# Expert layer of a two-block network: one-hots of two tokens side by side, an earlier first split, gate loads tied to weight loads, and padding between tiles

## The chip, the cores and the metric

The kernel runs on one core of one Trainium2 chip. The metric is the device time of one launch in microseconds (us). A core has a matrix engine (TensorE, PE in the profile; PEld is its loading of stationary operands), a vector engine (VectorE, DVE), a scalar engine (ScalarE, ACT), GpSimd (POOL), and the queue from which nearly all transfers are issued (SyncE, SP). Each works through its own list of instructions in order; semaphores tie the lists together. Operands lie in an on-chip memory of 128 partitions (SBUF); an address below is a byte offset within a partition. Sums of products land in a second memory, PSUM.

## The reference, cut to what matters

256 tokens of width 1024 pass first through two layers of attention and a gated MLP, then through two layers of a second kind: a mixing sublayer and a layer of 16,384 experts ("PEER"). Everything is float32. The change lies in the expert layer:

```
q      = xn @ wq                       # 8 heads x 2 halves x 128
scores = q . sub_keys                  # 128 keys per half
16 best of each half -> 16 best of the sums -> expert numbers idx = 128*i + j, gate = softmax
act    = xn . u_tab[idx]               # 8 x 16 experts per token
y      = sum over them of gelu(act) * gate * v_tab[idx]
```

The kernel does not gather rows. It computes the products with all 16,384 rows of U, multiplies gelu of them by a table of gates that is zero for experts not chosen, and multiplies the result by all rows of V.

## The kernel before, in words

**Weights.** Every large matrix comes in pieces of 128 x 1024 floats. `weights` (line 146) issues one transfer of 512 KB into one of three buffers `wx`, ACT rounds it to a short float `wh` (`split`, line 140) and DVE subtracts to get the rest `wl`; there are four buffers of each. A product x*w is three matmuls: high by high, low by high, high by low (`mm3`, line 134). PE, ACT and DVE work on different pieces; a buffer is written again when PE has read it. Transfers are issued from the SP queue in one order, so a transfer that waits for its buffer holds up those behind it.

**The expert layer (`peer`, line 1036).** After the choice of experts has begun (`select`, line 1187), U is done in two halves of 32 steps. A step (`u_step`) takes two pieces of U: 2 x 8 blocks x 3 = 48 matmuls, each with a 128 x 128 block of the piece as the stationary operand and 256 tokens as the moving one. ACT takes gelu of the sums into `at0` (first half) or `at1` (second). Beside the first half the rest of the choice runs (`rank`), woven in by `weave`.

**Gates.** For tokens 0 to 127 the gates are scattered by POOL into a table in HBM (`scatter_gates`, line 202), which has been cleared by 64 writes from a tile of zeros (`clear_gates`); later it comes back in 64 loads of 128 KB (`load_gates`, line 220), and DVE multiplies `at` by each. For tokens 128 to 255 they are built on the chip, four tokens at a time, in 32 builds (`build`): DVE compares a row of 0 to 127 with the chosen i (tile `oi`) and j (`oj`), multiplies `oj` by three parts of the gate (`og`), and for each of the four tokens PE multiplies `oi` by `og` in three bf16 matmuls of 128 x 128. The four tokens are interleaved: a token's column lies every fourth element, 8 bytes apart. DVE multiplies `at0` and what there is of `at1` by the result; ACT copies the rest to `at1`, and a later `u_step` multiplies its gelu by it (tile `y`). In the second half of U every step is followed by one build.

**V.** After the last build `first_split` loads two gates, multiplies, and splits the first chunk of `at` into `eh` and `el`; then 64 steps `v_step` follow, each with two pieces of V and 2 x 4 x 3 = 24 matmuls, with 128 x 128 of `eh` or `el` stationary and 512 columns of `wh` or `wl` moving. In the middle of a step `v_split` prepares the next chunk and asks for the gate two chunks on. The framework under the kernel orders each engine's list itself, by what could be ready; only stated dependencies bind it. The gate loads depend on the scatter and on a free buffer out of three.

**Where tiles lie.** Pools are laid out one after the other from both ends, the tiles of a pool in the order of their first use. By the sizes in the code, with the addresses that the program was given: `wx` from 20704, `wh` from 32992, `wl` from 49376, each buffer 4096 long, so every buffer of weights starts at 32 modulo 64. In the expert layer `xh` and `xl` (8 blocks of 256 floats, 1024 bytes each) start at 212960 and 221152, also 32 modulo 64, and `eh`, `el` of V too. In the second mixing sublayer `yh` starts at 113376 in layer 0 (32 modulo 64) and at 111616 in layer 1 (0 modulo 64); in the first block's MLP `gh` and `gl` start at 0 modulo 64.

Of the kernel before, what the change touches and what calls it, by code (L numbers as in the profile page):

```python
# [20 lines left out]
T = 256  # L21
# [26 lines left out]
OUT_ORDER = (4, 6, 7, 3, 0, 1, 5, 2)  # L48
WX, WH, WL = 3, 4, 4

# [5 lines left out]
LAG, TAIL, AHEAD, HOLD = 4, 2, 2, (2, 6)  # L56
SIDE_Q, SIDE_S = 2500, 2800
UQ_SIZES = [768, 512]
# [3 lines left out]
class Net:  # L62
    def __init__(self, tc, a, out, ctx, dbg=None):
        self.tc, self.nc, self.a, self.out, self.dbg = tc, tc.nc, a, out, dbg or {}
        self.n = 0
        self.queue = []
        self.act_set, self.act_pre, self.act_ops = None, None, []
        pool = tc.tile_pool
        self.cp = ctx.enter_context(pool(name="cp", bufs=1))
        self.wp = ctx.enter_context(pool(name="wp", bufs=1))  # L70
        self.gctx = ctx
        self.pp = ctx.enter_context(pool(name="pp", bufs=1, space=bass.MemoryType.PSUM))
        self.big = [self.pp.tile([128, 2, T], F32, name=f"big{b}", tag=f"big{b}", bufs=1) for b in range(4)]
# [391 lines left out]
    def out_tokens(self, units, first, last, then=None):  # L465

        for b in range(4):
            tk, s = slice(b % 2 * 128, b % 2 * 128 + 128), slice(b // 2 * 512, b // 2 * 512 + 512)
            for n, ((h, l), (xh, xl)) in enumerate(units):
                end = last and n == len(units) - 1  # L470
                self.mm(self.bank(b), xh[:, tk], h[:, s], first and n == 0, False)
                self.mm(self.bank(b), xl[:, tk], h[:, s], False, False)
                self.mm(self.bank(b), xh[:, tk], l[:, s], False, end)
            if then is not None:
                then(b)
# [560 lines left out]
    def peer(self, l):  # L1036
# [3 lines left out]
        with ExitStack() as ctx:  # L1040
            ip = ctx.enter_context(self.pool("pi"))
            idx = self.t(ip, [128, 128], U32, tag="idx")
            gs = [self.t(ip, [128, 8, 16], tag=f"gs{tt}") for tt in range(2)]
            iT, jT = (self.t(ip, [128, 128], BF16, tag=n) for n in ("iT", "jT"))
            gT = self.t(ip, [128, 3, 128], BF16, tag="gT")
            io = self.t(ip, [128, 128, 4], BF16, tag="io")
            for _ in self.clear:
# [20 lines left out]

            def build(g):


                t0, done = 124 - 4 * g, 2 * g + 2
                oi, oj = (self.t(self.op, [128, 128, 4], BF16, tag=n, bufs=2) for n in ("oi", "oj"))
                og = self.t(self.op, [128, 3, 128, 4], BF16, tag="og", bufs=2)
                self.tt(oi, io, iT[:, None, t0:t0 + 4].to_broadcast([128, 128, 4]), OP.is_equal)
                self.tt(oj, io, jT[:, None, t0:t0 + 4].to_broadcast([128, 128, 4]), OP.is_equal)
                self.tt(og, oj[:, None].to_broadcast([128, 3, 128, 4]),
                        gT[:, :, None, t0:t0 + 4].to_broadcast([128, 3, 128, 4]), OP.mult)
                yield 1900
                ps = self.ps([128, 4, 128])  # L1080
                for k in range(4):
                    for n in range(3):
                        self.mm(ps[:, k], oi[:, :, k], og[:, n, :, k], k == 0 and n == 0, n == 2)
                ps = ps.rearrange("p t j -> p j t")
                t0 += 128
                a0, a1 = at0[:, :, t0:t0 + 4], at1[:, :, t0:t0 + 4]
                self.tt(a0, a0, ps[:, :64], OP.mult)
                self.tt(a1[:, :done], a1[:, :done], ps[:, 64:64 + done], OP.mult)
                if done < 64:
                    self.copy(a1[:, done:], ps[:, 64 + done:])  # L1090
                yield 700

            parts, loaded = {}, {}

            def g_load(n):
                if n < 64:
                    loaded[n] = self.load_gates(l, n, early)

            def v_split(n, pool):

                if n < 64:
                    g_load(n + 2)
# [3 lines left out]
                    self.split(h, low, a)  # L1106
                    parts[n] = [(h[:, m], low[:, m]) for m in range(2)]

            def first_split():
                for n in range(2):  # L1110
                    g_load(n)
                v_split(0, early)

# [26 lines left out]
            with self.pool("pn") as npool:  # L1140
# [5 lines left out]
                self.xctx.close()  # L1146
                self.open_xs()
                pool = sctx.enter_context(self.pool("pk", "right"))
# [7 lines left out]
                self.copy(io16, it[:, 0:16, None].to_broadcast([128, 16, 128]))  # L1156
                self.copy(io, it[:, :, None].to_broadcast([128, 128, 4]))
# [12 lines left out]
            self.hctx.close()  # L1170
# [8 lines left out]
            vctx = ExitStack()  # L1179
            vp = vctx.enter_context(self.pool("pv", "right"))  # L1180
            for half, at in enumerate((at0, at1)):
                weave(lambda jp: v_step(at, jp, half), iter(()), 0)
            vctx.close()
        if l < DEPTH - 1:
            self.open_xs()

    def select(self, l, pool, w, lead, normed, io16, gs, idx, turned):
# [63 lines left out]
        def rest_of_ranks():  # L1251
            yield from normed
            pend.sort(key=lambda x: x[0])
            for tt in range(2):
# [15 lines left out]
                bt = best[tt]  # L1270
                g = gs[tt]
                self.tt(g, bt, bt[:, :, 0:1].to_broadcast([128, 8, 16]), OP.subtract)
# [265 lines left out]
```

## Time and profile before

| what | value |
|---|---|
| median of 2 runs | 2615.31 us (2614.23 to 2616.39) |
| the profiled execution, its own time | 2614.9 us |
| its span, first to last instruction | 2613.0 us |
[...]
| PE busy / DVE busy / ACT busy / POOL busy | 2560.8 / 1835.9 / 1383.7 / 463.4 us |
| transfers | 470.95 MB, 180 GB/s over the span |

A matmul's recorded duration includes the pipeline, and matmuls overlap: what a matmul costs is the distance of its start from the next one's. The chain of waits shows this best: it merges a run of matmuls into one line with its length and count, and length by count is the distance. The lines of a helper such as `mm` (L132), `copy` (L118) and `tt` (L121) carry many different operations; the names behind them tell which.

### The profile page before, as it was taken

Reading aid. Unit: us, or ns where it says so; the run is one execution under the profiler, and the core shown is the slowest. Engines: PE = TensorE matmul, PEld = TensorE weight load, DVE = VectorE, ACT = ScalarE, POOL = GpSimd, SP = SyncE. Lnnn points to the kernel's source line nnn. Section 1 sums busy time; section 2 is a strip of 40 time slices with the busy share of each in tenths; the row PEclk is TensorE's granted clock in tenths of the full one; section 3 lists DMA queues with packets and bytes.
Section 4 is the critical chain, followed back from the end, with each engine's and each line's share of the span. In section 5 each row is a group of like instructions: output and inputs, shape, how many; then the busy total and the mean of one; then the engine's idle time right before and its main releaser. Section 6 shows DMA issues by size and latency. Waiting matters only on the chain.

```text
span 2613.0 us, 46153 instructions
## 1 busy us (share of the span) xinstructions
PE 2560.8 (98%) x18042; PEld 2366.2 (91%) x18042; DVE 1835.9 (70%) x3511; ACT 1383.7 (53%) x2128; POOL 463.4 (18%) x261
## 2 busy tenths in 40 slices
PE   8999999999999999999999999999999999999999
PEld 7799997999999999999878888999999999878887
DVE  6688777877887995666665555877994666675555
ACT  6565566655676554444444444776554443344443
POOL 0000000000000077773000000000178772000000
PEclk9999999999999999999999999999999999999999
DMA  8756652566535576665576666635576665676664
GB/s 281 235 179 192 183 174 79 153 192 183 175 116 185 170 185 186 149 150 149 193 249 203 194 194 193 185 107 187 173 191 179 148 150 148 212 248 194 194 194 158
DMA packets 195098, 470.95 MB, mean 180 GB/s; under 512 B 54644, under 2 KB 89588, under 8 KB 193856
## 3 DMA queue, kind: packets, MB, share of 16 engines
q1 hardware_dynamic: 158016, 467.86, 56.9%
q0 software_dynamic: 36864, 0.15, 3.6%
q8 instruction: 141, 2.31, 0.3%
q14 instruction: 77, 0.63, 0.1%
HBM read 447.86 MB, written 20.05 MB: 179 GB/s over the span
## 4 chain that ended last, share of the span: by engine, by line
PE 85%; DMA 6%; DVE 6%; ACT 2%; issue 1%; SPq 0%; ACTq 0%; DVEq 0%
PE pj L132 46%; PE big L132 31%; PE ps L132 7%; DMA gate<-gates 4%; DVE wl L121 2%; DMA wx<-in_w 1%; ACT wh L118 1%; PE ps L573 1%; DVE el L121 1%; DVE xn L124 0%; DVE at L121 0%; DVE xT L121 0%; DMA wx<-in_wq 0%; DVE xl L124 0%; DVE c L124 0%
## 5 line engine op out<-in xcount | busy, mean ns | idle before, releaser
L118 ACT ACTIVATE wh<-wx 128x1024 fp32r<-128x1024 f32 (+1 forms) x800 | 844.4, 1057 | 898.7 <-PE pj L132 356.1
L121 DVE TENSOR_TENSOR wl<-wx,wh 128x1024 fp32r<-128x1024 f32 (+1 forms) x800 | 975.0, 1220 | 453.8 <-ACT wh L118 446.4
L132 PE MATMUL pj<-xh,wh 128*128 128x256 f32 x3136 | 897.3, 286 | 10.5 <-ACT wh L118 7.9
L132 PE MATMUL pj<-xl,wh 128*128 128x256 f32 x3136 | 889.6, 284 | 3.3 <-DVE xl L124 2.7
L132 PE MATMUL pj<-xh,wl 128*128 128x256 f32 x3136 | 889.1, 284 | 3.8 <-DVE wl L121 3.8
L209 POOL DMA_INDIRECT gates<-gs,idx x256 | 462.9, 1808 | 1712.6 <-DVE idx L129 1591.8
L132 PEld LDWEIGHTS pj<-xh,wh 128*128 128x128 f32 x3136 | 601.2, 192 | 12.8 <-ACT wh L118 8.3
L132 PEld LDWEIGHTS pj<-xl,wh 128*128 128x128 f32 x3136 | 600.5, 191 | 7.9 <-DVE xl L124 6.5
L132 PEld LDWEIGHTS pj<-xh,wl 128*128 128x128 f32 x3136 | 599.9, 191 | 6.6 <-DVE wl L121 5.7
L132 PE MATMUL big<-wh,el 128*128 128x512 f32 x1024 | 402.1, 393 | 10.4 <-DVE el L121 10.3
L132 PE MATMUL big<-wh,eh 128*128 128x512 f32 x1024 | 400.0, 391 | 11.6 <-ACT eh L118 11.6
L132 PE MATMUL big<-wl,eh 128*128 128x512 f32 x1024 | 399.9, 390 | 0.0
L132 PEld LDWEIGHTS big<-wh,el 128*128 128x128 f32 x1024 | 193.1, 189 | 58.4 <-DVE el L121 19.2
L132 PEld LDWEIGHTS big<-wh,eh 128*128 128x128 f32 x1024 | 193.0, 189 | 52.6 <-ACT eh L118 12.2
L132 PEld LDWEIGHTS big<-wl,eh 128*128 128x128 f32 x1024 | 193.1, 189 | 39.6
L121 DVE TENSOR_TENSOR at<-at,ps 128x256 f32<-128x256 f32 (+20 forms) x128 | 45.1, 352 | 131.6 <-PE ps L132 131.6
L132 PE MATMUL ps<-og,oi 128*128 128x128 bf16 x768 | 101.5, 297 | 0.0
L132 PE MATMUL big<-gh,wh 128*128 128x256 f32 x352 | 99.1, 282 | 0.0
L132 PE MATMUL big<-gl,wh 128*128 128x256 f32 x352 | 98.9, 281 | 0.0
L132 PE MATMUL big<-gh,wl 128*128 128x256 f32 x352 | 98.8, 281 | 0.0
L121 DVE TENSOR_TENSOR at<-at,gate 128x256 f32<-128x256 f32 x128 | 52.9, 422 | 58.4 <-DMA gate<-gates 58.0
L121 DVE TENSOR_TENSOR el<-at,eh 128x512 fp32r<-128x512 f32 x128 | 87.2, 684 | 0.0
(355 smaller groups left out, 3309.0 us busy)
## 6 DMA issues: line engine op xcount, KB each, us to landing
wx<-in_u SPq DMA_DIRECT2D x256, 512.0 KB
wx<-in_v SPq DMA_DIRECT2D x256, 512.0 KB
wx<-in_wm SPq DMA_DIRECT2D x132, 512.0 KB
wx<-in_w SPq DMA_DIRECT2D x88, 512.0 KB
gates<-zero SPq DMA_DIRECT2D x128, 128.0 KB
wx<-in_wo SPq DMA_DIRECT2D x32, 512.0 KB
wx<-in_wq SPq DMA_DIRECT2D x32, 512.0 KB
gate<-gates SPq DMA_DIRECT2D x128, 128.0 KB
```

Of the source, the lines that this page charges most:

```text
L118: return self.nc.scalar.activation(out, in_, AF.Copy)
L121: return self.nc.vector.tensor_tensor(out, a, b, op=op)
L132: return self.nc.tensor.matmul(ps, w, x, start=start, stop=stop, skip_group_check=True)
L209: d = self.nc.gpsimd.indirect_dma_start(flat, IndirectOffsetOnAxis(ap=idx[:, p:p + 1], axis=0), g[:, p:p + 1], None, compute_op=OP.add).ins
L573: self.nc.tensor.transpose(tp[:, kt, qt * 128:(qt + 1) * 128], p[:, qt, kt * 128:(kt + 1) * 128], self.ident)
```

## The change

- **Interleaving.** The one-hots hold two pairs of two tokens, [128, 2, 128, 2], so that a token's column lies every second element, 4 bytes apart; `og` is made in two halves. The numbers of instructions: one DVE multiplication more per build, the same 12 matmuls.
- **Order.** The builds are a generator `builds`, woven into the second half of U like `rank` into the first, at 3100 ns of work per step (a build yields 2750); `pairs` and `built` count what is done. gelu of the tokens that have a gate already is now written back to PSUM and multiplied from there. When the builds are through, `first_split` follows in the same weave, with gate 0 in a tile of its own; gates 1 and 2 are asked for when V begins.
- **Gate loads** get a dependency on the last weight load before them in the program (`fetched`), which orders them behind it in the SP queue.
- **Padding.** A lead of 288 bytes before `wx`, `zero` half as large (its copies read it twice), each pair of weight buffers a tag of its own with 32, 32, 64, 0 bytes behind `wl`; 64 bytes behind each of the 8 blocks of `xh` and `xl` in the expert layer, and 480 or 448 bytes above them; `eh`, `el` in blocks of 136 floats, 544 bytes; 32 bytes above V's pool. By the same rule of layout `wx` then starts at 20480 and the four pairs `wh`, `wl` at 0, 32, 64 and 128 modulo 512; `xh` starts at 211456 in layer 0 (0 modulo 64) and at 211488 in layer 1 (32 modulo 64), with blocks 1088 bytes apart. Tiles of the left pools move down by 96 bytes.

```diff
+LEAD, PADS = 288, (32, 32, 64, 0)
+VP = (32, 32)
-SIDE_Q, SIDE_S = 2500, 2800
+SIDE_Q, SIDE_S, SIDE_G = 2500, 2800, 3100
...
+        self.t(self.wp, [128, LEAD // 4], tag="lead")
...
-            self.nc.sync.dma_start(x[:, :tot], ap[:, off:off + tot])
+            self.fetched = self.nc.sync.dma_start(x[:, :tot], ap[:, off:off + tot]).ins
...
-                h = self.t(self.wp, [128, 1024], F32R, tag="wh", bufs=WH)
-                l = self.t(self.wp, [128, 1024], F32R, tag="wl", bufs=WL)
+                b = self.units % 4
+                h, l = (self.t(self.wp, [128, 1024 + n // 4], F32R, tag=x + "abcd"[b]) for x, n in (("wh", 0), ("wl", PADS[b])))
+                self.units += 1
...
-        self.zero = self.t(self.cp, [128, 2, 128], tag="zero")
+        self.zero = self.t(self.cp, [128, 128], tag="zero")
...
-            self.nc.sync.dma_start(self.gates[l][:, j:j + 2], self.zero)
+            self.nc.sync.dma_start(self.gates[l][:, j:j + 2], self.zero[:, None].to_broadcast([128, 2, 128]))
...
-        g = self.t(pool, [128, 2, 128], tag="gate", bufs=3)
+        g = pool if n == 0 else self.t(pool, [128, 2, 128], tag="gate", bufs=3)
         d = self.nc.sync.dma_start(g, self.gates[l][:, 2 * n:2 * n + 2]).ins
+        self._dep(d, self.fetched)
...
-    def open_xs(self):
+    def open_xs(self, gap=0, below=0):
...
-        self.xh, self.xl = (self.t(pool, [128, 8, T], F32R, tag=n) for n in ("xh", "xl"))
+        self.xh, self.xl = (self.t(pool, [128, 8, T + gap // 4], F32R, tag=n)[:, :, :T] for n in ("xh", "xl"))
+        if below:
+            self.t(pool, [128, below // 4], tag="below")
...
-            def u_step(at, jp, tb=0):
+            def u_step(at, jp):
...
-                a = at[:, 2 * jp:2 * jp + 2]
-                self.act(a[:, :, :T - tb], ps[:, :, :T - tb], AF.Gelu_apprx_tanh)
-                if tb:
-                    y = self.t(self.op, [128, 2, 128], tag="y", bufs=2)[:, :, :tb]
-                    self.act(y, ps[:, :, T - tb:], AF.Gelu_apprx_tanh)
-                    self.tt(a[:, :, T - tb:], a[:, :, T - tb:], y, OP.mult)
+                a, n = at[:, 2 * jp:2 * jp + 2], T - built[0]
+                self.act(a[:, :, :n], ps[:, :, :n], AF.Gelu_apprx_tanh)
+                if built[0]:
+                    self.act(ps[:, :, n:], ps[:, :, n:], AF.Gelu_apprx_tanh)
+                    self.tt(a[:, :, n:], a[:, :, n:], ps[:, :, n:], OP.mult)
-            def build(g):
...
+            def builds(pairs):
+                for t0 in range(124, -1, -4):
+                    oi, oj = (self.t(self.op, [128, 2, 128, 2], BF16, tag=n, bufs=b) for n, b in (("oi", 2), ("oj", 1)))
+                    chosen = lambda x: x[:, t0:t0 + 4].rearrange("p (a t) -> p a t", t=2)[:, :, None].to_broadcast([128, 2, 128, 2])
+                    for o, x in ((oi, iT), (oj, jT)):
+                        self.tt(o, io[:, None].to_broadcast([128, 2, 128, 2]), chosen(x), OP.is_equal)
+                    ps = self.ps([128, 4, 128])
+                    for a in range(2):
+                        og = self.t(self.op, [128, 3, 128, 2], BF16, tag="og", bufs=2)
+                        self.tt(og, oj[:, a:a + 1].to_broadcast([128, 3, 128, 2]),
+                                gT[:, :, None, t0 + 2 * a:t0 + 2 * a + 2].to_broadcast([128, 3, 128, 2]), OP.mult)
+                        for k in range(2):
+                            for n in range(3):
+                                self.mm(ps[:, 2 * a + k], oi[:, a, :, k], og[:, n, :, k], a == 0 and k == 0 and n == 0,
+                                        n == 2)
+                    yield 2000
...
+                    built[0] += 4
+                    yield 750
...
-                    h, low = (self.t(pool, [128, 2, T], F32R, tag=x, bufs=1 + (n > 0)) for x in ("eh", "el"))
+                    h, low = (self.t(pool, [128, 2, 2, 136], F32R, tag=x, bufs=1 + (n > 0))[:, :, :, :128] for x in ("eh", "el"))
...
-                for g in range(32):
-                    u_step(at1, g, 4 * g)
-                    for _ in build(g):
-                        pass
-            early = ctx.enter_context(self.pool("pf"))
-            first_split()
+                weave(u_second, builds(pairs), SIDE_G, first_split)
...
+            for n in (1, 2):
+                g_load(n)
```

## Rows read from the trace of the kernel before

**Rows 1.** Page, part 1: each engine's busy time, share, instructions.
```profile
PE 2560.8 (98%) x18042; PEld 2366.2 (91%) x18042; DVE 1835.9 (70%) x3511; ACT 1383.7 (53%) x2128; POOL 463.4 (18%) x261
```

**Rows 2.** Chain of waits: start us, length us, what; the expert layers.
```profile
862.38 126.00 PE pj L132 x1050
...
1053.47 5.75 PE pj L132 x48
1059.22 1.43 PE ps L132 x12
...
1373.81 265.28 PE big L132 x1169
```

**Rows 3.** Windows: stretch, its length, busy us of each engine, clock, DMA share, GB/s.
```profile
1053.00:1268.00 215.00, 215.00 (x1800) 213.14 (x1798) 142.98 (x237) 87.94 (x150) 119.34 (x72) 1.00 0.59 148
1268.00:1374.00 106.00, 94.58 (x430) 75.95 (x428) 70.94 (x116) 44.34 (x54) 0.00 (x0) 0.97 0.76 243
1374.00:1640.00 266.00, 266.00 (x1178) 220.42 (x1178) 149.69 (x149) 129.70 (x148) 0.00 (x0) 1.00 0.62 196
```

**Rows 4.** Timeline of PE, U's last matmul to V's first in layer 0.
```profile
1274.32 0.28 PE L132 MATMUL pj<-xh,wl 128*128 128x256 f32 x1
1274.45 1.58 PE L132 MATMUL ps<-og,oi 128*128 128x128 bf16 x12
1281.82 1.22 PE L132 MATMUL big<-wh,eh 128*128 128x512 f32 x2 [5.80 <-ACT eh L118]
1282.84 0.63 PE L132 MATMUL big<-wh,el 128*128 128x512 f32 x1
1283.27 0.63 PE L132 MATMUL big<-wl,eh 128*128 128x512 f32 x1
1283.69 0.63 PE L132 MATMUL big<-wh,el 128*128 128x512 f32 x1
```

**Rows 5.** Waits and the queue's own, 1268 to 1374: total us, times, longest.
```profile
DVE at L121 <- DMA gate<-gates: 29.3, 24, 3.0
PE big L132 <- DVE el L121: 5.6, 8, 1.8
...
SPq L154 <- DVE at L121: 16.2, 14, 1.5
```

**Rows 6.** Chain of waits, V's beginning and steady part in layer 1; a gate's landing.
```profile
2243.97 5.50 DMA gate<-gates
...
2250.64 12.90 PE big L132 x47
...
2342.22 266.66 PE big L132 x1175
```

**Rows 7.** Groups by line, 1053 to 1268: count, busy us, mean ns, idle before.
```profile
L132 PEld LDWEIGHTS pj<-xh,wh 128*128 128x128 f32 x480 | 91.8, 191 | 0.0
L121 DVE TENSOR_TENSOR wl<-wx,wh 128x1024 fp32r<-128x1024 f32 x60 | 73.4, 1223 | 9.8 <-ACT wh L118 9.2
L132 PE MATMUL ps<-og,oi 128*128 128x128 bf16 x360 | 47.7, 297 | 0.0
L132 PEld LDWEIGHTS <-oi 128*128 128x128 bf16 x358 | 38.1, 118 | 1.8
L121 DVE TENSOR_TENSOR og<-oj,gT 128x1536 bf16<-128x1536 bf16 x30 | 28.5, 949 | 0.0
L121 DVE TENSOR_TENSOR at<-at,ps 128x256 f32<-128x256 f32 (+30 forms) x60 | 20.9, 348 | 61.7 <-PE ps L132 61.7
L121 DVE TENSOR_TENSOR oi<-io,iT 128x512 bf16<-128x512 bf16 x30 | 12.5, 418 | 0.0
L121 DVE TENSOR_TENSOR at<-at,y 128x8 f32<-128x8 f32 (+28 forms) x29 | 8.0, 276 | 0.0
```

**Rows 8.** Timeline of POOL, the last scatter of layer 0.
```profile
1202.51 1.54 POOL L209 DMA_INDIRECT gates<-gs,idx  x1 [0.30 <-issue]
```

**Rows 9.** Chain of waits: output products of the mixing sublayer, layers 0 and 1.
```profile
795.02 8.17 PE big L132 x68
...
1762.67 7.96 PE big L132 x68
```

**Rows 10.** Chain of waits in the first block's MLP: up (pj), then down (big).
```profile
205.10 2.84 PE big L132 x24
207.94 5.75 PE pj L132 x48
```

More of the change, by code (lines that the diff above doesn't have):

```diff
@@ L48 @@
 OUT_ORDER = (4, 6, 7, 3, 0, 1, 5, 2)
-WX, WH, WL = 3, 4, 4
+WX = 3
+LEAD, PADS = 288, (32, 32, 64, 0)
 ATT = "ka nk nq va x2 A1 rk uq x0 a1 uk A0 w1 w0 a0 B0 vc x1 B1 w2 b1 C1 c1 b0 C0 c0 D0 D1 d0 d1"
@@ L66, in __init__ @@
         self.queue = []
+        self.units = 0
         self.act_set, self.act_pre, self.act_ops = None, None, []
@@ L467, in out_tokens @@
         for b in range(4):
-            tk, s = slice(b % 2 * 128, b % 2 * 128 + 128), slice(b // 2 * 512, b // 2 * 512 + 512)
+            s = slice(b // 2 * 512, b // 2 * 512 + 512)
             for n, ((h, l), (xh, xl)) in enumerate(units):
                 end = last and n == len(units) - 1
-                self.mm(self.bank(b), xh[:, tk], h[:, s], first and n == 0, False)
-                self.mm(self.bank(b), xl[:, tk], h[:, s], False, False)
-                self.mm(self.bank(b), xh[:, tk], l[:, s], False, end)
+                self.mm(self.bank(b), xh[:, b % 2], h[:, s], first and n == 0, False)
+                self.mm(self.bank(b), xl[:, b % 2], h[:, s], False, False)
+                self.mm(self.bank(b), xh[:, b % 2], l[:, s], False, end)
             if then is not None:
@@ L1042, in peer @@
             idx = self.t(ip, [128, 128], U32, tag="idx")
-            gs = [self.t(ip, [128, 8, 16], tag=f"gs{tt}") for tt in range(2)]
+            gs = self.t(ip, [128, 8, 16], tag="gs")
             iT, jT = (self.t(ip, [128, 128], BF16, tag=n) for n in ("iT", "jT"))
             gT = self.t(ip, [128, 3, 128], BF16, tag="gT")
-            io = self.t(ip, [128, 128, 4], BF16, tag="io")
+            io = self.t(ip, [128, 128, 2], BF16, tag="io")
+            first = self.t(ip, [128, 2, 128], tag="gate")
+            built = [0]
             for _ in self.clear:
@@ L1061, in u_step @@
                     self.proj_fm(w, ps[:, m])
-                a = at[:, 2 * jp:2 * jp + 2]
-                self.act(a[:, :, :T - tb], ps[:, :, :T - tb], AF.Gelu_apprx_tanh)
-                if tb:
-                    y = self.t(self.op, [128, 2, 128], tag="y", bufs=2)[:, :, :tb]
-                    self.act(y, ps[:, :, T - tb:], AF.Gelu_apprx_tanh)
-                    self.tt(a[:, :, T - tb:], a[:, :, T - tb:], y, OP.mult)
-            def build(g):
[L1072 to L1091, printed above, removed]
@@ new lines, in u_step @@
+                a, n = at[:, 2 * jp:2 * jp + 2], T - built[0]
[19 more added lines that the diff above has]
+                    yield 2000
+                    ps, done = ps.rearrange("p t j -> p j t"), 2 * pairs[0]
+                    a0, a1 = (x[:, :, 128 + t0:132 + t0] for x in (at0, at1))
+                    self.tt(a0, a0, ps[:, :64], OP.mult)
+                    self.tt(a1[:, :done], a1[:, :done], ps[:, 64:64 + done], OP.mult)
+                    if done < 64:
+                        self.copy(a1[:, done:], ps[:, 64 + done:])
+                    built[0] += 4
+                    yield 750
@@ L1096, in g_load @@
                 if n < 64:
-                    loaded[n] = self.load_gates(l, n, early)
+                    loaded[n] = self.load_gates(l, n, vp)
             def v_split(n, pool):
                 if n < 64:
-                    g_load(n + 2)
+                    if n:
+                        g_load(n + 2)
                     a = (at0, at1)[n // 32][:, 2 * (n % 32):2 * (n % 32) + 2]
                     self.tt(a[:, :, :128], a[:, :, :128], loaded.pop(n), OP.mult)
-                    h, low = (self.t(pool, [128, 2, T], F32R, tag=x, bufs=1 + (n > 0)) for x in ("eh", "el"))
-                    self.split(h, low, a)
+                    h, low = (self.t(pool, [128, 2, 2, 136], F32R, tag=x, bufs=1 + (n > 0))[:, :, :, :128] for x in ("eh", "el"))
+                    self.split(h, low, a.rearrange("p m (t c) -> p m t c", c=128))
                     parts[n] = [(h[:, m], low[:, m]) for m in range(2)]
[L1109 to L1112, printed above, removed]
             def v_step(at, jp, half):
@@ L1146, in peer @@
                 self.xctx.close()
-                self.open_xs()
+                self.open_xs(64, (480, 448)[l])
                 pool = sctx.enter_context(self.pool("pk", "right"))
@@ L1156, in peer @@
                 self.copy(io16, it[:, 0:16, None].to_broadcast([128, 16, 128]))
-                self.copy(io, it[:, :, None].to_broadcast([128, 128, 4]))
+                self.copy(io, it[:, :, None].to_broadcast([128, 128, 2]))
             self.xs = self.xh, self.xl
@@ L1162, in peer, with u_second, first_split @@
             at1 = half_acts()
-            with self.pool("po") as self.op:
-                for g in range(32):
-                    u_step(at1, g, 4 * g)
-                    for _ in build(g):
-                        pass
-            early = ctx.enter_context(self.pool("pf"))
-            first_split()
+            early = ctx.enter_context(self.pool("pf"))
+            pairs = [0]
+            def u_second(jp):
+                u_step(at1, jp)
+                pairs[0] += 1
+            def first_split():
+                loaded[0] = self.load_gates(l, 0, first)
+                v_split(0, early)
+            with self.pool("po") as self.op:
+                weave(u_second, builds(pairs), SIDE_G, first_split)
             self.hctx.close()
@@ L1180, in peer @@
             vp = vctx.enter_context(self.pool("pv", "right"))
+            for n in (1, 2):
+                g_load(n)
             for half, at in enumerate((at0, at1)):
                 weave(lambda jp: v_step(at, jp, half), iter(()), 0)
+            self.t(vp, [128, VP[l] // 4], tag="below")
             vctx.close()
@@ L1270, in rest_of_ranks @@
                 bt = best[tt]
-                g = gs[tt]
+                g = gs if tt == 0 else self.t(pool, [128, 8, 16], tag="g")
                 self.tt(g, bt, bt[:, :, 0:1].to_broadcast([128, 8, 16]), OP.subtract)
```

## The prediction

> **What bounds it.** I read the page's first part, then the chain of waits, then windows by stage, then the timeline and the waits where a window showed idle time. PE is busy 98% of the span [rows 1], so the question is what each matmul costs and where PE stands still. The chain gives the cost: in U's first half 1050 matmuls in 126.00 us, 120.0 ns each; in the second half 48 in 5.75 us and then 12 of a build in 1.43 us, 119 ns each, 7.18 us a step; in V 1169 in 265.28 us, 226.9 ns each [rows 2]. [...] The windows show where PE stands still: nowhere in U's second half (215 of 215 us), nowhere in V's steady part, but 106 us at V's beginning have 94.58 us of PE and a clock of 0.97 [rows 3].
>
> **Builds.** A build's matmul streams 128 columns, yet takes the 119 ns of 256 columns [rows 2]. Both cover 1024 bytes: 128 x 8 or 256 x 4. I read this as a limit by bytes passed over. With tokens interleaved in twos, 128 columns cover 512 bytes. [...] I take 62, half of the 120 of rows 2 and a little, since the address pattern is then that of floats side by side. 2 x 32 x 12 = 768 matmuls x 57 ns = 44 us, all on the path, since PE sets the step. The weight load's 118 ns [rows 7] need not bind: loads of 128 floats take 191 ns [rows 7] while their matmuls start 120 apart, so loads overlap.
> [...]
>
> **U's second half beside PE.** A step shrinks to 5.75 + 12 x 0.062 = 6.49 us. DVE had 142.98 us in 215 [rows 3], 4.8 per step. A line through `oi` (512 elements, 418 ns) and `og` (1536, 949) gives 0.55 us for half an `og`, so two cost 1.10 instead of 0.95 [rows 7]. A build is then 0.42 + 0.42 + 1.10 + 2 x 0.35 = 2.64 us; 3100 against 2750 ns of side work makes 1.13 builds a step; with two splits of 1.22 and the product of 0.28 that is 5.7 us of 6.49. It fits, and consecutive DVE instructions overlap a little beyond that. What must not stay is DVE's wait for a build's matmuls, 61.7 us in 30 steps, 2.06 each [rows 7]: the weave moves the second part of a build behind the next step's splits. If all of it stays, steps take 5.7 + 2.06 = 7.8 us, 1.3 us more than forecast over 28 steps and two layers, 72 us. I take nothing, and keep 72 for the range. gelu written back to PSUM holds its bank until DVE's product; the other bank covers it for a step.
>
> **V's beginning.** In layer 0 U's last builds start at 1274.45 and V at 1281.82, so beside 1.43 us of build PE stands idle 5.9 us [rows 4]; a gate's landing takes 5.5 of it (layer 1's row) [rows 6]. [...] From 1281.82 to 1373.81 the 1536 - 1169 = 367 matmuls take 92.0 us against 83.3 at 226.9 ns: 8.7 us lost. In layer 1, by the same count, 361 take 91.6 against 81.9: 9.7 lost [rows 6]. Both layers: 2 x 5.9 + 18.4 = 30 us. Their cause is that all 64 gate loads are pulled into these first steps: DVE waits for gates 24 times, up to 3.0 us, and weight loads wait in the SP queue behind gates whose buffers DVE has not freed [rows 5]. With each gate load behind a weight load, this goes. The first split falls into U: builds end after 32 x 2750/3100 = 28.4 steps, leaving three to hide gate 0, the product and the split. Scattering ends at 1202.5 [rows 8], and step 29 begins near 1053.47 - 7.18 + 29 x 6.49 = 1234.5 [rows 2], so SP, which runs a few steps ahead, need hardly wait for it. Next late is gate 1: its load can start only when U has released its activations, together with 1 MB of `xT`, and took 5.5 us there; with product and split (0.44 + 0.64 + 0.7) it is ready 7.3 us after U, while step 0 lasts 5.45. I charge 2 us per layer. Net 26 us; bounds 0 and 30.
>
> **Padding.** PE reads a moving operand and the next stationary one at once. Nearly everywhere both start at the same place modulo 64 and the distance stands at 120 ns. The mixing layer has a trial of the other case: the same 68 output products take 8.17 us in layer 0, with `yh` and `wh` both at 32 modulo 64, and 7.96 in layer 1, with `yh` at 0 [rows 9]: 120.1 and 117.1 ns. In the MLP, `gh` against `wh` (apart by 32) gives 2.84/24 = 118.3 beside 119.8 for `xh` against `wh` (equal) [rows 10]. So 1.5 to 3.1 ns for starts 32 apart; I take 2.2. How many matmuls gain: three of four weight buffers now differ by 32 from an operand at 32 modulo 64, one from an operand at 0. U of layer 0: 3072/4; U of layer 1: 3072 x 3/4; V, where blocks of 544 bytes alternate: half of 3072; all the rest, about 6960 less 1800 that had it: 3/4, less the quarter of those 1800 that lose it. About 8000 x 2.2 = 18 us. [...]
> [...]
>
> **Costed at nothing.** Gate clears read 512-byte rows twice; transfers have the engines for 0.59 to 0.62 of the time there [rows 3]. One DVE instruction more per build is counted above. In V a gate is asked for two steps, 10.9 us, ahead and lands in 5.5 [rows 6].
>
> **Sum.** 2614.9 (the profiled execution, 0.4 under the median) - 44 - 26 - 18 = 2527.
>
> **Rivals.**
> - *Padding does much more*, because multiples of 64 matter too: 2614.9 - 44 - 26 - 107 = 2438. For it: distances vary once starts differ. Against: in U equal starts give the same 120 whatever the block. Chance 0.17.
> - *Padding does nothing* beyond scatter: 2545. Against it stand rows 9. 0.12.
> - *Build matmuls stay at 119 ns*, being set by the weight load's 118 [rows 7] or by the step as such: 2571, within 2%. [...] 0.10.
> - *DVE sets the pace* in U's second half, with its old waits: up to 2599. 0.08.
> - *Slower: gates come late in every step.* The multiplication by a gate stands in DVE's list before splits of weights; a load held behind weight loads that wait for buffers lands after DVE gets there, PE runs out of `wl`, and this comes in 126 steps instead of some 30. The place is the gate load, the price up to the 3.0 us of rows 5. V's gain is gone and 2614.9 - 62 = 2553 is left; from 62/126 = 0.5 us per step it is slower than before, at 1.5 us it is 2742. For it: DVE's waits were of this kind. Against: 10.9 us of lead. 0.08.
> - The forecast, 2527: 0.45.
>
> **Chances.** About 2% either way is what a measurement of this kernel can tell from no change, 2563 being the line. Faster: most of the forecast and the first two rivals, 0.73. Within: the third, most of the fourth, a rest, 0.21. Slower 0.06. The range runs from the bound of padding to the DVE case, 2440 to 2590.
>
> **What would show it.** Builds: a line of 12 in the chain near 0.75 us and steps near 6.5. V: matmuls at 227 ns or less from its first, no idle of 5.8 us before it, gate waits gone from DVE's list. Padding: U's chain below 120 ns by more in layer 1 than in layer 0. I am wrong if 12 build matmuls still take 1.4 us, if DVE waits for gates all through V, or if U of layer 0 falls as far as that of layer 1.

## The result and the profile after

The changed kernel takes 2550.3 us (2548.9 to 2551.7) against 2615.3: ratio 0.976, interval 0.973 to 0.978. Forecast were 2527 in a range of 2440 to 2590, so direction and range held, and 65 us came where 88 were expected. The profiled execution after took 2548.9 us, its span is 2547.1.

The page's first part, after (engine, busy us, share of the span, instructions); compare [rows 1]:
```profile
PE 2510.7 (99%) x18042; PEld 2303.8 (90%) x18042; DVE 1830.6 (72%) x3575; ACT 1390.6 (55%) x2130; POOL 472.6 (19%) x261
```
PE lost 50 us of work in as many instructions, and 16 us of idling. The chain of waits after, the lines that answer to [rows 2, 6, 9] (start us, length us, what, count):
```profile
785.37 8.08 PE big L137 x68
...
852.70 123.82 PE pj L137 x1050
...
1047.08 5.70 PE pj L137 x48
1052.78 0.71 PE ps L137 x12
1053.49 5.73 PE pj L137 x48
...
1248.30 126.96 PE big L137 x540
...
1724.21 8.08 PE big L137 x68
...
1792.65 124.19 PE pj L137 x1050
...
2189.20 353.81 PE big L137 x1512
```
Length by count: U's matmuls fell from 120.0 to 117.9 ns in layer 0 and 118.3 in layer 1. A step of U's second half is 1053.49 - 1047.08 = 6.41 us instead of 7.18, of which 0.71 are the twelve matmuls of a build, 59 ns each instead of 119. V's matmuls rose from 226.9 to 234 ns, small stalls included.

The window after of V's beginning (columns as in [rows 3]):
```profile
1246.00:1354.00 108.00, 105.70 (x450) 85.53 (x451) 63.87 (x80) 49.78 (x57) 0.00 (x0) 0.98 0.65 208
```
V's beginning is nearly full where [rows 3] had 94.58 of 106 us. Two groups of U's second half (1047 to 1240) answer to [rows 7] (count, busy us, mean ns, idle before and its releasers):
```profile
L126 DVE TENSOR_TENSOR og<-oj,gT 128x768 bf16<-128x768 bf16 x58 | 31.9, 554 | 10.5 <-PE ps L137 9.6 <-issue 0.6 <-DVE oj L126 0.3
L126 DVE TENSOR_TENSOR at<-at,ps 128x256 f32<-128x256 f32 x30 | 12.4, 415 | 1.1 <-PE ps L137 1.0
```
Half an `og` takes the 0.55 us estimated, and of DVE's 61.7 us of waiting for PE's builds 10.6 are left (9.6 before `og`, 1.0 before `at`). PE's timeline from U to V's second step:
```profile
1239.27 0.28 PE L137 MATMUL pj<-xh,wlb 128*128 128x256 f32 x1
1239.39 0.40 PE L137 MATMUL big<-whc,eh 128*128 128x512 f32 x1
...
1244.74 0.39 PE L137 MATMUL big<-wld,eh 128*128 128x512 f32 x1
1248.30 2.08 PE L137 MATMUL big<-wha,eh 128*128 128x512 f32 x4 [3.17 <-ACT eh L123]
1250.18 0.63 PE L137 MATMUL big<-wha,el 128*128 128x512 f32 x1
1250.60 0.63 PE L137 MATMUL big<-wla,eh 128*128 128x512 f32 x1
```
V follows U without a gap, where [rows 4] had one. One step later PE waits 3.17 us for the split of gate 1's activations, then some matmuls start about 427 ns apart (1250.18, 1250.60): the granted clock from 1248.5 to 1251 is 0.50. The waits of layer 0's V (1240 to 1610) show what the forecast said would go:
```profile
DVE at L126 <- DMA gate<-gates: 129.9, 58, 2.8
```

For the comparison by parts I took the starts of all matmuls from each trace; sums over both layers, us, each kernel's profiled execution (e9's took 2510.6 us, 7.7 over the median; the experiments are told below). In the kernel before and in e2 the last build of a layer (1.4 and 0.7 us) stands behind U and is counted in the fourth row; elsewhere all builds lie in U:

| part | before | after | e1 | e2 | e4 | e8 | e9 | e10 | e11 |
|---|---|---|---|---|---|---|---|---|---|
| start to U of layer 0 | 860.4 | 850.5 | 856.7 | 856.0 | 856.5 | 855.5 | 856.6 | 842.7 | 842.3 |
| U, first halves | 371.6 | 365.8 | 371.6 | 371.5 | 352.2 | 371.6 | 362.7 | 358.0 | 353.4 |
| U, second halves | 456.6 | 412.6 | 417.2 | 414.5 | 403.0 | 417.2 | 401.2 | 401.6 | 401.7 |
| from U to V: last build, PE idle | 14.7 | 0 | 0 | 15.0 | 0 | 0 | 0 | 0 | 0 |
| V | 717.2 | 726.3 | 732.0 | 718.9 | 745.8 | 705.4 | 697.0 | 697.0 | 714.0 |
| V of layer 0 to U of layer 1 | 188.0 | 187.2 | 188.3 | 188.3 | 188.1 | 187.8 | 187.0 | 184.8 | 184.9 |
| V: distances over 260 ns, their excess over the usual one | 19.5 | 12.0 | 31.4 | 21.2 | 45.2 | 8.4 | 0.1 | 0.1 | 0.1 |
| median time of the runs | 2615.3 | 2550.3 | 2571.1 | 2570.7 | 2550.4 | 2545.5 | 2502.9 | 2487.2 | 2503.8 |

### The profile page after: what moved, and what is told of

The parts are those of the page before. It is cut to its first block, busy times and chain, and to the rows that moved or that the text cites. A ratio compares the mean times of both kernels' runs of the same rounds, so it can differ in the third digit from the quotient of the medians.

```text
span 2547.1 us, 46104 instructions
## 1 busy us (share of the span) xinstructions
PE 2510.7 (99%) x18042; PEld 2303.8 (90%) x18042; DVE 1830.6 (72%) x3575; ACT 1390.6 (55%) x2130; POOL 472.6 (19%) x261
## 4 chain that ended last, share of the span: by engine, by line
PE 87%; DMA 5%; DVE 5%; ACT 2%; issue 1%; SPq 0%; DVEq 0%; ACTq 0%
PE pj L137 47%; PE big L137 34%; PE ps L137 6%; DMA gate<-gates 3%; DMA wx<-in_w 1%; DVE wld L126 1%; DVE wlb L126 1%; PE ps L583 1%; DVE xn L129 1%; DVE xT L126 0%; DMA wx<-in_wq 0%; DVE xl L129 0%; DMA wx<-in_wm 0%; DVE c L129 0%; ACT whc L123 0%
## 5 line engine op out<-in xcount | busy, mean ns | idle before, releaser
L126 DVE TENSOR_TENSOR wlc<-wx,whc 128x1024 fp32r<-128x1024 f32 x200 | 244.4, 1222 | 102.0 <-ACT whc L123 94.8
L126 DVE TENSOR_TENSOR wla<-wx,wha 128x1024 fp32r<-128x1024 f32 x200 | 244.4, 1222 | 99.7 <-ACT wha L123 95.8
L126 DVE TENSOR_TENSOR wld<-wx,whd 128x1024 fp32r<-128x1024 f32 x200 | 243.2, 1216 | 58.1 <-ACT whd L123 57.7
L126 DVE TENSOR_TENSOR wlb<-wx,whb 128x1024 fp32r<-128x1024 f32 x200 | 243.2, 1216 | 54.0 <-ACT whb L123 53.5
L137 PE MATMUL pj<-xh,wha 128*128 128x256 f32 x792 | 227.7, 288 | 9.4 <-ACT wha L123 8.1
L126 DVE TENSOR_TENSOR at<-at,gate 128x256 f32<-128x256 f32 x128 | 54.0, 425 | 248.2 <-DMA gate<-gates 248.0
L137 PE MATMUL pj<-xh,whc 128*128 128x256 f32 x792 | 227.2, 287 | 1.2 <-ACT xh L116 1.1
L137 PE MATMUL pj<-xl,wha 128*128 128x256 f32 x792 | 224.5, 283 | 1.8 <-DVE xl L129 1.7
L137 PE MATMUL pj<-xh,wla 128*128 128x256 f32 x792 | 223.8, 283 | 1.9 <-DVE wla L126 1.9
L137 PE MATMUL pj<-xl,whc 128*128 128x256 f32 x792 | 223.6, 282 | 1.5 <-DVE xl L129 1.5
L137 PE MATMUL pj<-xh,wlc 128*128 128x256 f32 x792 | 223.2, 282 | 1.5 <-DVE wlc L126 1.5
```

The lines of the kernel that those rows point to most:

```text
L126: return self.nc.vector.tensor_tensor(out, a, b, op=op)
L137: return self.nc.tensor.matmul(ps, w, x, start=start, stop=stop, skip_group_check=True)
```

## Experiments

**m1: distance by itself.** This kernel leaves the network out and runs only series of 24 matmuls, each with a moving and a stationary operand at chosen addresses; it ran once.
```diff
+    for i in range(32):
+        series("s" + letters(i), 256, 24, [(0, 4 * i)])
+    for i in range(32):
+        series("l" + letters(i), 512, 24, [(0, 4 * i)])
...
+    for i, s in enumerate((1, 2, 4, 8)):
+        series("c" + letters(i), 128, 24, [(0, 0)], (b, c), (s, 1))
+        series("d" + letters(i), 128, 24, [(0, 0)], (b, c), (1, s))
```


> This kernel leaves out the network: it only runs series of 24 matmuls on random data, PE alone, and copies x to the output. Series: moving operand at a fixed address, stationary operand 0, 16, 32, ... 496 bytes further modulo 4096, for 256 and for 512 columns; alternating offsets; bf16 columns every 1, 2, 4 or 8 elements. Theory A (the two operands' start addresses collide): the distance between matmuls depends on the offset, about 120 ns for 256 columns where starts are equal modulo 64 and 113 to 118 elsewhere; alternating between offsets can be worse than either. Theory B (addresses do not matter to PE alone, what moved was contention with other engines' writes): one value for all offsets, at or below 120. bf16: by the bytes-covered theory 128 columns take about 57 ns at steps of 1 and 2 elements, 107 to 119 at 4, about 215 at 8, and it is the moving operand's step that counts; by the rival (the load of the stationary operand) its step counts.

The chain of waits of m1: first 256 columns with the stationary operand 0, 64, 128 and 320 bytes beyond the moving one, then 512 columns at 0, 64 and 256, then bf16 matmuls of 128 columns with the moving columns 2, 4, 8 and 16 bytes apart (caa to cad) and with the stationary ones 8 apart (dac):
```profile
19.22 2.88 PE saa L43 x24
...
30.61 2.72 PE sae L43 x24
...
41.88 2.88 PE sai L43 x24
...
75.99 2.72 PE sau L43 x24
...
109.99 5.47 PE laa L43 x24
...
132.10 5.59 PE lae L43 x24
...
198.93 5.44 PE laq L43 x24
...
418.65 1.34 PE caa L43 x24
...
422.71 1.39 PE cab L43 x24
...
428.26 2.79 PE cac L43 x24
431.04 1.34 PE dac L43 x24
...
437.99 5.45 PE cad L43 x24
```
By 24: 256 columns take 120 ns at 0, 113 at 64, 120 at 128, and repeat after 256 bytes. 512 columns take 227 to 228 at 0 and 233 at 64. So distance counts, but modulo 256 rather than 64, and the best distance for one width is not the best for the other. The builds' part is confirmed: the bytes that the moving operand passes over set the time from 4 bytes a column on (2 bytes apart 56 ns, 4 apart 58, 8 apart 116, 16 apart 227), and those of the stationary one at 8 apart do not (56).

**e1, e2, e3: parts undone.** e1 is the change without its padding, e2 the kernel before with the interleaved layout alone, e3 the change without the order of gate loads behind weight loads.
```diff
e1
-        self.t(self.wp, [128, LEAD // 4], tag="lead")
...
-                self.open_xs(64, (480, 448)[l])
+                self.open_xs()
...
e2 (on before)
-                oi, oj = (self.t(self.op, [128, 128, 4], BF16, tag=n, bufs=2) for n in ("oi", "oj"))
+                oi, oj = (self.t(self.op, [128, 2, 128, 2], BF16, tag=n, bufs=2) for n in ("oi", "oj"))
...
e3
-        self._dep(d, self.fetched)
```


> The changed kernel with all padding undone (no lead, one tag each for wh and wl, zero at full size, xh, xl, eh, el without gaps, nothing above the pools); order, interleaving and gate loads as in the change. Theory A (padding shortens distances in U and elsewhere by about 2 ns but lengthens V's from 226.9 to 232, because V's operands were in a good relation before): V back at 226.9, U back at 120.0, total about +5 us against the change, 2556; in parts, V -16, first block and mixing +10, U +11. Theory B (V's longer distance comes from something else, such as gate loads now spread over V): V stays at 232 and the total is about 2572.

> The kernel before with only the interleaving in twos: one-hots [128, 2, 128, 2], og in two halves, same order of steps and builds, same addresses of weights and activations as before. Theory A (a build's matmul is limited by the bytes its columns cover): 12 matmuls take about 0.70 us instead of 1.43, steps 6.45 instead of 7.18, the total 2615 - 64 x 0.70 = 2570. Theory B (the gain of U's second half came from the weave): steps stay near 7 us, total above 2600.

> The changed kernel without the dependency of gate loads on weight loads; all else as changed. Theory A (the dependency is what spreads the gate loads): loads are pulled together at V's beginning again, PE loses about 9 us per layer there instead of 5 to 7, total +5 to +9 us, about 2557. Theory B (DVE's 248 us of waiting for gates in the changed kernel cost more than the jam did): total falls by up to 10 us.

e1: 2571.1 us, ratio to before 0.984 (0.982 to 0.985). e2: 2570.7, 0.983 (0.982 to 0.985). e3: 2926.8, 1.119 (1.117 to 1.121).

e2 came as its theory A had it; its chain shows a build at 58 ns a matmul:
```profile
1047.41 0.70 PE ps L132 x12
```
In e1 the distances of theory A came (227 ns in V, 120 in U), but not its time of 2556.

The parts add up: before to e2 -44 (interleaving), e2 to e1 0 (order), e1 to after -21 (padding). The surprise is the 0: the gap from U to V closed (-15.0, of which 1.4 are builds that moved into U), and V grew by 13.1. The waits of e1's V in layer 0 (1250 to 1620):
```profile
DVE at L125 <- DMA gate<-gates: 134.9, 58, 3.0
ACT wh L122 <- DMA wx<-in_v: 124.4, 78, 2.2
...
PEld big L136 <- DVE el L125: 17.4, 43, 0.9
```
By the starts of its matmuls V runs, after its first two steps, at 5.44 us a step up to the fifteenth; from there on PE starves a little in nearly every step, and a step takes 5.71 us on average. One step in the timeline shows a ring:
```profile
1405.24 0.43 SPq L227 DMA_DIRECT2D gate<-gates  x1
...
1405.49 0.19 PEld L136 LDWEIGHTS big<-wh,el 128*128 128x128 f32 x1 [0.25 <-DVE el L125]
...
1406.60 4.12 SPq L158 DMA_DIRECT2D wx<-in_v  x2
...
1408.80 0.42 DVE L125 TENSOR_TENSOR at<-at,gate 128x256 f32<-128x256 f32 x1 [2.23 <-DMA gate<-gates]
...
1409.14 1.22 DVE L125 TENSOR_TENSOR wl<-wx,wh 128x1024 fp32r<-128x1024 f32 x1
...
1410.77 0.43 SPq L227 DMA_DIRECT2D gate<-gates  x1
```
The gate is issued at 1405.24 behind the weights and takes about 3.7 us to land (the median of the three in 1400 to 1412); DVE stands 2.23 us before the product that needs it; the split of weights sits behind that product in DVE's list; the second weight load waits for the split and is issued by 1410.72; the next gate goes after it. This turn is 5.53 us; on average the gates of this V are issued 5.71 us apart from the eighth on, and 24 matmuls at 226.9 ns are 5.45. So PE uses up a lead in V's first steps and then goes at the ring's pace. In the kernel after, the issues lie 5.65 us apart and 24 matmuls at 232 ns are 5.57, so the same ring is nearly hidden: DVE's wait is 129.9 us there too, but PE's weight loads wait for `el` only 15 times, 4.4 us in all, instead of 43 times and 17.4. Hence V is 5.7 us shorter over both layers after than in e1 although its matmuls are 5 ns slower.

e3 missed in both theories. Without the order the loads of gates are placed far ahead and SP's queue stands at the unfinished scatter. Its own waits, whole run:
```profile
SPq L229 <- DMA gates<-gs,idx: 381.3, 8, 188.2
```
The 190 us per layer are weight loads that stand behind it. The order is needed.

**e4, e5, e6, e7: each fault mended by itself, on e1.** e4 puts U's activations 64 bytes lower; e5 keeps the order for gates 0 to 2 alone; e6 is both; e7 is e6 with gate 1 loaded in U.
```diff
e4
-                self.open_xs()
+                self.open_xs(0, 64)
e5
-        self._dep(d, self.fetched)
+        if n < 3:
+            self._dep(d, self.fetched)
e7 (with e4 and e5)
-        g = pool if n == 0 else self.t(pool, [128, 2, 128], tag="gate", bufs=3)
+        g = pool if n < 2 else self.t(pool, [128, 2, 128], tag="gate", bufs=3)
...
-                loaded[0] = self.load_gates(l, 0, first)
+                for n in range(2):
+                    loaded[n] = self.load_gates(l, n, first[:, n])
```


> This is e1 (the change without its gaps and pads) with one thing more: in U the activations lie 64 bytes lower, so that each weight tile begins 64 bytes after the activations modulo 256 instead of at the same place. Theory A (from m1: what counts is the distance modulo 256, and 64 is best for 256 columns): U's matmuls fall from 119.6 to about 113.3 ns, 6144 of them in two layers by 6.3 ns are 39 us, V stays at about 366, time 2532 us (2525 to 2540). Theory B (the prediction's: starts equal modulo 64 are bad, 32 bytes apart good): 64 bytes are no distance, so U stays at 119.6 ns and the time at e1's 2571 us. Theory C (vector work or weight loads take over once matmuls are faster): the matmuls fall, but the first and the second half of U do not by as much, time 2545 to 2565 us.

> This is e1 with the rule that a load of gates waits in the queue for the latest weights kept only for gates 0, 1 and 2, and dropped for 3 to 63. Theory A (the rule closes a ring in V: gates wait behind weights on SyncE, VectorE waits for the gates, the split of weights waits behind that on VectorE, and the next weights wait for that split; one turn is 5.5 us or more, over the 5.45 us of 24 matmuls at 227 ns): V falls from 366.9 and 365.1 to 358 to 361 us, the wait of matmuls for el nearly goes, and the time is 2554 to 2560 us. Theory B (V without padding is held by the weight transfers themselves, about 1.15 MB per step): V stays at 365 to 367 us and the time within 3 us of e1's 2571. Theory C: loads are issued so early that the queue stands still, as in e3: slower than 2600 us.

> e4 and e5 together (no gaps or pads, U at a distance of 64 modulo 256, the rule of the queue kept for gates 0 to 2 alone). Theory A: the two gains add up, U at 113 ns and V at 227 ns with few stalls: 2571 - 39 - 14 = 2518 us (2508 to 2528). Theory B (the faster of the two only moves the wait): no better than the better one of e4 and e5 by more than 5 us.

> e6 with gate 1 loaded during U, as gate 0 is, into memory of its own. Theory A (the late gate 1 costs its wait of about 3.5 us and then some eight matmuls at half the clock, 5.3 us per layer in the kernel after): e6 less 8 to 11 us. Theory B (what gate 1 no longer costs, gate 2 costs one step later, since it can only be loaded once U has ended): e6 less 0 to 3 us. Theory C (a transfer of gates during U delays the weights there): no gain, up to 5 us slower.

e4: 2550.4 us, 0.975 (0.974 to 0.977). U's first halves fell by 19.4 us and the second by 14.2, not far from the 39 of theory A; its time (2525 to 2540) did not come, since V grew by 13.8, which no theory had: its first steps lose more, and its excess went from 31.4 to 45.2 us. The ring is the likely cause of part of it: in e4 the gates are issued 5.78 us apart and V's steps from the fifteenth on take 5.79. Why its turn is longer than in e1 is not shown.

e5: 2564.6, 0.981 (0.980 to 0.983); half of what theory A gave. Its SP queue in V's first third, one weight load and then two gates, again and again:
```profile
1306.06 0.33 SPq L158 DMA_DIRECT2D wx<-in_v  x1
1307.00 1.58 SPq L227 DMA_DIRECT2D gate<-gates  x2
1309.40 0.33 SPq L158 DMA_DIRECT2D wx<-in_v  x1
```
All gates rush through in the first 18 steps, four in a step that needs one, as in the kernel before [rows 5]. The windows show the price and that nothing is left to pay afterwards:
```profile
1300.00:1356.00 56.00, 50.52 (x212) 39.15 (x213) 38.54 (x64) 23.56 (x27) 0.00 (x0) 1.00 0.80 247
1370.00:1500.00 130.00, 130.00 (x575) 107.66 (x574) 72.71 (x72) 62.89 (x72) 0.00 (x0) 1.00 0.62 194
```
e6: 2535.1, 0.970 (0.968 to 0.971), 17 us over its forecast; its V, 725.9 us, is as long as that of e5, so the same reason is likely. e7: 2535.4, 0.970 (0.968 to 0.971), no gain: the stalls of V's first two steps are gone in its trace, but both gates now wait in SP's queue for the last scatter while U runs. SP's timeline, e7:
```profile
1201.69 4.52 SPq L158 DMA_DIRECT2D wx<-in_u  x2
1216.81 0.80 SPq L227 DMA_DIRECT2D gate<-gates  x2
```
Ten microseconds without an issue cost U some 6 us in that layer (its second half takes 206.3 us there, in e6 200.5).

**e8: the ring cut.** One rule on e1: the product by a gate follows the latest split of weights in DVE's list.
```diff
-                    self.tt(a[:, :, :128], a[:, :, :128], loaded.pop(n), OP.mult)
+                    m = self.tt(a[:, :, :128], a[:, :, :128], loaded.pop(n), OP.mult)
+                    if n:
+                        self._dep(m.ins, self.low.ins)
```


> This is e1 (the change without gaps and pads) with one rule more: VectorE multiplies by gate n only after the split of the latest weights then asked for, so a late gate no longer holds up the split that the next weights, and behind them the next gate, wait for. Theory A (the ring of gate, multiplication, split, weights, gate is what holds V at 5.7 us a step in e1): the wait of matmuls for el in V nearly goes, V falls from 366.9 and 365.1 to 356 to 361 us, most of the 16 us of stalls per layer but for the 5 us at the first two steps; time 2553 to 2561 us. Theory B (the gates' own way through the queue and memory takes that long): V stays within 2 us of e1's and the time at 2568 to 2574 us.

2545.5 us, 0.974 (0.973 to 0.976): V falls by 26.6 us, more than theory A had. It is the clearest run of the study: no load is added, moved earlier or made smaller, and 25.6 us come back. The gates are now issued 5.44 us apart, at PE's own pace, instead of 5.71. The waits of its V (layer 0, 1247 to 1602) hold no gate; what PE still waits for is step 1:
```profile
PE big L136 <- ACT eh L122: 3.2, 1, 3.2
```
So the change without any padding, with this one rule, takes no longer than the change as it was made (2550.3; the intervals of the two ratios overlap).

**e9, e10, e11: put together.** e9 adds to e8 the distance of e4, gates 0 and 1 loaded in U two weight blocks later than in e7, and gates asked for three steps ahead, from four buffers. e10 lowers `xh` and `xl` by 64 bytes in all stages. e11 is e10 with V's split activations at the change's pitch.
```diff
e9
-                        g_load(n + 2)
+                        g_load(n + 3)
...
+                if jp == 30:
+                    first_split()
e10
-    def open_xs(self, gap=0, below=0):
+    def open_xs(self, gap=0, below=64):
e11
-                    h, low = (self.t(pool, [128, 2, 2, 128], F32R, tag=x, bufs=1 + (n > 0)) for x in ("eh", "el"))
+                    h, low = (self.t(pool, [128, 2, 2, 136], F32R, tag=x, bufs=1 + (n > 0))[:, :, :, :128] for x in ("eh", "el"))
```


> No gaps or pads, U at a distance of 64 modulo 256 (e4), multiplications pinned (e8), gate 1 loaded during U as in e7, both early loads two weight blocks further back in the queue so that they do not wait there for the last scatter, and gates loaded three steps ahead from four buffers in place of two from three. Theory A: V has neither the stalls of its first two steps nor e5's crowding of steps 7 to 18, so V is 350 to 356 us per layer against 363 in e6, and U as in e6: 2535 - 16 = 2519 us (2510 to 2528). Theory B (the 1 MB of kept x loaded as V begins, and the weights behind it, make the stalls whatever the gates do): V stays at 360 or more, 2530 to 2540 us.

> e9 with the activations xh and xl 64 bytes lower in the other stages too (projections of both blocks; some 3100 matmuls of 256 columns that stood at no distance, 119.6 ns). Theory A (distance modulo 256 decides, 64 is best): these fall to 113 to 116 ns, 11 to 20 us, nearly all of it on the path: e9 less 9 to 20 us. Theory B (there the vector work or the weights set the pace, or the distance does not matter): e9 within 4 us.

> e10 with V's split activations at the pitch of 544 bytes that the change gave them, so that they stand at 0, 32, 64 and 96 and more bytes from the weights modulo 256 and no longer all at 0. Theory A (for 512 columns no distance is the best, 227 against 232 ns): V's matmuls go to 231 to 233 ns, 3072 times 5 ns: e10 plus 13 to 18 us. Theory B (the prediction's: equal starts modulo 64 are bad, 32 apart good; half of the parts stand 32 apart): V's matmuls get faster by 2 ns, e10 less 5 to 8 us.

e9: 2502.9 us, 0.957 (0.956 to 0.959); e10: 2487.2, 0.951 (0.950 to 0.953); e11: 2503.8, 0.958 (0.956 to 0.960). e9 came below its 2510 to 2528, with 348.5 us of V a layer where 350 to 356 were expected; what each of its four edits gave was not run by itself. e10 and e11 came as their theory A had it. The chain of e10, U's first halves, and V of layers 0 and 1:
```profile
844.70 119.02 PE pj L136 x1050
964.04 62.19 PE pj L136 x528
...
1221.31 346.82 PE big L136 x1530
...
1757.03 123.67 PE pj L136 x1050
1881.03 59.86 PE pj L136 x528
...
2136.30 348.19 PE big L136 x1536
```
V is one unbroken run at 226.7 ns: the 19.5 us of stalls of the kernel before are gone. In e11 the line of V reads:
```profile
1220.95 355.30 PE big L136 x1530
```
232.2 ns, and the kernel is 16.6 us slower: what V's pitch of 544 bytes costs where nothing hides it. By ratios e10 beats the changed kernel by 0.9511 / 0.9757, 2.5%; the two were not timed in one session.

## Why the prediction was right or wrong

**Builds: right.** Forecast -44 at 62 ns a matmul; e2 measured -44 in time and -42 in U's second halves. By the starts, the last matmul of a build included, one costs 55.8 ns where it cost 111.6. The rule behind it, bytes passed over by the moving operand, holds in m1 from 4 bytes a column on (58, 116 and 227 ns at 4, 8 and 16 bytes), and the stationary operand's span up to 8 bytes a column does not matter there (56 ns). The rival of 119 ns by the weight load is out.

**DVE beside U: right.** DVE is busy for 139.62 of the 185 us from 1048 to 1233, 4.9 us a step where 5.7 were forecast and 6.41 are there, and of the wait of [rows 7] a sixth is left, which delays no matmul of U there; the rival with 72 us did not come.

**V's beginning: wrong, and the step that failed is the cover of the gates in V.** The gap went as forecast: the 14.7 us held 2.9 of builds and 11.9 of idling, where 11.8 were forecast, and all idling is gone. But -26 was the net, and by e2 to e1 the whole of the order was worth 0: these 26 us, less 3 that padding gave more, are the 23 that the result lacks of the forecast. I had costed V's steady part at nothing because "a gate is asked for two steps, 10.9 us, ahead and lands in 5.5" [rows 6]. It is asked for two steps ahead in the program, not in time: in e1's step above the gate that DVE takes at 1408.80 was issued 3.6 us earlier, about its way of 3.7. The new order puts the issue behind weight loads that wait for a split that stands behind the previous product. That is the mechanism of my last rival, at a third of the price from which it decides: e1's excess of 31.4 us less e8's 8.4, over 128 steps, is 0.18 us a step, where the rival needed 0.5. That it is a ring rather than slow transfers is shown by e8, which cuts it in DVE's list alone. With the ring cut the order is worth what the forecast had for it: from e2 to e8 it is 25 us, against 26. So the sum for V's beginning was right, and the term put at nothing was the one that failed. My test "if DVE waits for gates all through V" came true (248.0 us over the run); in the kernel after the time hardly showed it, since slower matmuls covered most of it.

Gate 1 was charged 2 us a layer; it cost 3.2 us of standing and 1 to 2 us by matmuls 427 ns apart, at a granted clock of 0.50. Loading it early paid nothing in e7, where U lost as much; in e9, which asks two weight blocks later, V's first steps are free of stalls and U keeps its time.

**Padding: right in size, wrong in mechanism.** Forecast -18, measured e1 to after -21. But the rule, starts equal modulo 64 bad and 32 apart good, is wrong, and its own test failed: U of layer 0 fell as far as that of layer 1 (117.9 and 118.3 ns), and `yh` takes 8.08 in both layers where [rows 9] differed. With m1's table the numbers come out: blocks 1088 bytes apart against weights 512 apart run through four distances that differ by 64, so from a pair at 0 U takes 120.0, 117.9, 120.0 and 113.3 ns (distances 0, 192, 128, 64), mean 117.8, and from a pair at 32 118.3, 116.7, 120.0 and 117.1, mean 118.0, in either layer. By matmul durations the padding gives 6.2 us ahead of U, 5.8 and 4.6 in U, 1 elsewhere, and takes back 3072 x 5.4 ns = 16.6 in V: about -1. The other 20 are an accident, and it was luck that the forecast of 18 met them: without the padding V would be faster than the ring allows, so slower matmuls cost nothing there. (That -1 is worked out; padding with the ring cut was run for V's pitch alone, e11.) I had costed V's padding as a gain of half its matmuls, with the opposite sign. No run shows the 107 us that the first rival's 2438, and with it the range's lower end, take off for padding: m1 has 6.7 ns between the worst and the best distance at 256 columns (120.0 and 113.3), the 226.9 of V before stand at the low end of its 226.7 to 234.2 at 512, and the distances that were run gave 33.6 us in U (e1 to e4) and 16.1 in the stages around it (e9 to e10).

**The rivals.** "Padding does much more" came closer than I thought: not with the change's own pads, but 64 bytes in the right place gave e4's U and e10's other stages what the gaps did not. The order without its rule of the queue (e3) would have been the slower case, by a mechanism, a queue standing at a scatter, that the forecast weighed only for the new order, where SP "need hardly wait for it".

## What to carry to other kernels

A load's lead is counted from its place in its queue, and one has to ask what that place waits for: follow gate, product, split, buffer, weight load, gate round to the start and compare the turn (5.71 us on average in e1) with the step (5.45). A wait that costs nothing today may be covered only by another fault, so removing the fault shows no gain until the wait is cut too; undo both. Addresses belong to the tuning of matmuls here, but a distance has to be measured for each width of the moving operand, since the best for 256 columns was a bad one for 512 (64 bytes: 113 ns, where 0 has 120, and 233 ns, where 0 has 228).

## What the runs showed of the hardware that was not expected

- Time of a matmul against the stationary operand's distance from the moving one repeats after 256 bytes: 113 to 120 ns at 256 columns, 227 to 234 at 512; the best distance is 64 bytes for 256 columns and 0 for 512. e4, which moves only the activations, gives U 113.4 ns as well (402 matmuls in 45.59 us of its chain), so it is the distance that counts and not the address of one operand. What makes it so is open.
- At a distance of 64, U's matmuls run in one of two paces with the same addresses, 113.3 or 117.8 ns, and keep it from one break to the next: in e10 1050 matmuls in 119.02 us in layer 0 and in 123.67 in layer 1, and the 528 after them in 62.19 and 59.86, the other way round. At 0 and in V I saw one pace only. The slow stretches of these first halves cost e10 4.65 + 2.33 = 7.0 us. What chooses the pace is open.
- After 3.2 us of standing in V's second step matmuls started 426 or 427 ns apart for two to four microseconds, at a granted clock of about 0.5 (in the kernel after 0.50 from 1248.5 to 1251); in e8's second layer the same standing was not followed by it (1512 matmuls in 343.04 us, 226.9 ns each), and in e9 to e11, where nothing stands, it is not seen in V.
